# Pairing the first network's up product, and making a third of the later modulations' sums during attention, in a two-layer decoder trunk

## The chip, the cores and the metric

The kernel runs on one core of one Trainium2 chip, as one program and one launch. The metric is device time in microseconds, from the runs of the program on the chip; lower is better. Beside the plain runs there is one profiled execution, from which every row in this document comes. Engine names in the rows are PE (TensorE, matmuls), PEld (TensorE, weight loads), DVE (VectorE), ACT (ScalarE), POOL (GpSimd) and SP (SyncE, which here only issues transfers).

## The reference

One sequence of 256 tokens with 2048 channels goes through two layers. Layer 0 mixes tokens by a causal convolution module, layer 1 by causal stick-breaking attention with 16 heads of 128. Behind each mixer stands a gated network with 5632 inner channels, whose up product is followed by a depthwise causal convolution of width 3. Each of these four sub-layers has its own norm and its own shift, scale and gate, a modulation made from one conditioning vector `c`:

```python
def ada_ln(c, w, b):
    mod = jax.nn.silu(c) @ w + b
    shift, scale, gate = jnp.split(mod, 3, axis=-1)

def conv_ffn(h, up_w, dw_w, dw_b, down_w):
    u = causal_depthwise_conv(h @ up_w, dw_w, dw_b)
    gt, val = jnp.split(u, 2, axis=-1)
    return (jax.nn.silu(gt) * val) @ down_w

for i in range(DEPTH):
    shift, scale, gate = ada_ln(c, mix_mod_w[i], mix_mod_b[i])
    h = rms_norm(x, mix_norm_g[i]) * (1.0 + scale) + shift
    y = conformer_conv_module(...) if i == 0 else stick_breaking_mixer(...)
    x = x + gate * y
    shift, scale, gate = ada_ln(c, ffn_mod_w[i], ffn_mod_b[i])
    h = rms_norm(x, ffn_norm_g[i]) * (1.0 + scale) + shift
    x = x + gate * conv_ffn(h, ffn_up_w[i], ffn_dw_w[i], ffn_dw_b[i], ffn_down_w[i])
return rms_norm(x, final_norm_g)
```

All of it is float32.

## The kernel before, in words

**Tiles.** Activations stand with channels on the 128 partitions and the 256 tokens along the free axis, so `x` is 16 tiles of 128 x 256. A weight matrix is cut into blocks of 128 x 128. Eight blocks make a piece of 512 KB, which SP fetches into a tile `raw`, five pieces ahead of its use. The list `stream` holds the pieces of all products in the order in which they are used.

**Two-part products.** Nearly every product is made with operands split into a high and a low part. ScalarE copies a piece of weights into `wh` (L241), VectorE makes `wl = raw - wh` (L245), three pieces ahead, into a ring of four buffers. The activations have such halves too: `h` for a network's or the attention's input, `g` for the gated inner values, `o` for the heads' outputs. A block then needs weights-high times activation-high, weights-high times activation-low, and weights-low times activation-high. `gemm` has two forms of it:

- three matmuls of 256 columns (L301, L302, L303), all into the same 256 columns of a PSUM bank;
- where `both` is given, two matmuls (L296, L297). The two halves of an activation lie in one tile, and an access pattern reads both as 512 columns, so that one matmul multiplies weights-high by both. The bank then holds the high product in its columns 0 to 255 and the low one in columns 256 to 511, and whoever reads the bank adds them. The weights-low matmul goes into the first 256 columns.

Before the change the first network's up product uses the first form, except that its first four columns of blocks come from another function, `product`, with 258 columns. The first network's down product, attention's products and all of the second network use the second form. The last column of each down product uses the first form in both networks.

**What a network does with its up product.** For a column of 128 channels that is done, `up_done` calls `conv3`: in the second form ScalarE copies the low product out of PSUM (L996) and VectorE adds the high one to it (L997). Then ScalarE applies the first tap (L1000), and VectorE the other two (L1003, twice). When both columns of a pair are there, ScalarE applies SiLU, VectorE multiplies (L1015), ScalarE copies the high half (L1017) and VectorE makes the low half `g` (L1018). Each network runs as up00a, up00b, up01a, down00, up01b, down01 (up10a and so on in the second): 4, 40, 2 and 42 columns of up with 16 blocks each, and two down products of 16 columns with 22 blocks each. In down01 each finished column is added to `x` (L1025 on GpSimd, L1029 on VectorE), squared for the next norm (L401, L405), and scaled and split for the next product (L457, L458).

**Modulations.** The later modulations (network 0's gate, all of the attention's and network 1's) are 1 MB tiles of weights, each 128 outputs x 2048 inputs. GpSimd issues the load into a tile `mraw` (L328), and VectorE multiplies it by the conditioning vector and sums along the row in one instruction (L335). The generator `mods1` takes one step per load, and in a step, once its ring of buffers is full, it also issues the sum of the oldest one. The ring has five buffers in the first network, three elsewhere. Generators like this one stand in the list `fill`; after every piece of a product, `tick` adds the product's rate to a credit, and each whole credit advances `fill` by a step. The table `RATES` gives the rate and the starting credit by the product's name. Before the change one generator with 96 tiles runs in the first network, and one with 16 (network 1's gate) in the second. Attention runs with an empty `fill`.

**Attention.** For each group of four heads come the value product, then the query and key products. Each head's own work is a generator in `side` which advances a step per piece. With `q` and `k` done, PE makes the scores (L1106), ScalarE three functions of them, VectorE `e` and `lg` (L1115, L1116), GpSimd two masks (L1118), ScalarE and VectorE the halves `mh` and `ml` (L1127), PE the cumulative sums (L1131 to L1134), VectorE a subtraction (L1135), ScalarE an exponential, GpSimd two masks (L1139), and PE the product with the values (L1144, L1145). The output product `o` follows; each of its finished columns is added to `x` (L1210, twice) and prepared for network 1 (L401, L457, L458). If the shift of network 1's modulation is there, two columns of it are also split (L468 on ScalarE, L469 on VectorE, 128 x 2); if not, that is made up for in one go as soon as it is.

**Order.** PE, VectorE and ScalarE each run their own instructions in the order in which a scheduler placed them; engines meet at semaphores only. An instruction that waits holds up everything behind it on its engine.

## Time and profile before

| what | value |
| --- | --- |
| median of 3 runs | 2295.64 us (2295.11 to 2296.51) |
| the profiled execution's own time | 2295.03 us |
| its span, first to last instruction | 2293.3 us |
| mean granted TensorE clock over the span | 0.998 |
| bytes moved | 603.16 MB, mean 263 GB/s |
| weights' transfers (SP's queue), share of 16 DMA engines | 57.8% |
| modulations' transfers (GpSimd's queue), share of 16 DMA engines | 16.2% |
| modulation sums (L335) | 152, of which 96 between 431 and 1155 us |

The stages in the span: the convolution module to 407 us, the first network to 1155 us, attention with its output product to 1545 us, the second network to the end.

How to read it: a matmul's duration includes its way through the array, and the next one starts well before it ends. Busy time of PE is therefore no measure of its pace; the time of a stage divided by its number of blocks is. A stage is cut at the first matmul of its product. In the answers by stretch, the number behind an engine's busy time is the count of instructions that touch the stretch.

### The profile page before, as it was taken

Reading aid. Unit: us, or ns where it says so; the run is one execution under the profiler, and the core shown is the slowest. Engines: PE = TensorE matmul, PEld = TensorE weight load, DVE = VectorE, ACT = ScalarE, POOL = GpSimd, SP = SyncE. Lnnn points to the kernel's source line nnn. Section 1 sums busy time; section 2 is a strip of 40 time slices with the busy share of each in tenths; the row PEclk is TensorE's granted clock in tenths of the full one; section 3 lists DMA queues with packets and bytes.
Section 4 is the critical chain, followed back from the end, with each engine's and each line's share of the span. In section 5 each row is a group of like instructions: output and inputs, shape, how many; then the busy total and the mean of one; then the engine's idle time right before and its main releaser. Section 6 shows DMA issues by size and latency. Waiting matters only on the chain.

```text
span 2293.3 us, 37838 instructions
## 1 busy us (share of the span) xinstructions
PE 2259.4 (99%) x14466; PEld 2013.9 (88%) x14466; DVE 1791.2 (78%) x2502; ACT 1218.4 (53%) x1930; POOL 411.6 (18%) x535
## 2 busy tenths in 40 slices
PE   7999999999999999999999999999999999999997
PEld 5888678999998999998898888889888888888887
DVE  7689968989998899999975655778899755777654
ACT  2056655755544455555465555657555544555553
POOL 4058713200002100003421100122000010000031
PEclk9999999999999999999999999999999999999999
DMA  9988798789899989888765555566787665666663
GB/s 396 417 337 305 272 364 348 279 299 336 334 332 347 347 316 331 338 325 306 291 192 161 167 174 174 166 192 232 238 286 283 194 192 185 192 192 185 193 191 111
DMA packets 139144, 603.16 MB, mean 263 GB/s; under 512 B 15441, under 2 KB 15569, under 8 KB 115153
## 3 DMA queue, kind: packets, MB, share of 16 engines
q1 hardware_dynamic: 120242, 464.42, 57.8%
q0 software_dynamic: 18720, 136.32, 16.2%
q8 instruction: 113, 1.85, 0.3%
q14 instruction: 69, 0.57, 0.1%
HBM read 598.58 MB, written 2.10 MB: 262 GB/s over the span
## 4 chain that ended last, share of the span: by engine, by line
PE 87%; DVE 6%; DMA 4%; ACT 1%; issue 1%; POOL 0%; DVEq 0%; SPq 0%; ACTq 0%; POOLq 0%
PE ps L296 33%; PE ps L297 17%; PE ps L302 9%; PE ps L301 9%; PE ps L303 9%; PE ps L694 5%; DMA mraw<-in_mt_mix 3%; DVE mraw L335 3%; DVE wl L245 1%; PE ps L1185 1%; PE ps L1184 1%; PE ps L1186 1%; PE ps L585 1%; DMA mraw<-in_mt_ffn 1%; DMA raw<-in_w_pw 1%
## 5 line engine op out<-in xcount | busy, mean ns | idle before, releaser
L245 DVE TENSOR_TENSOR wl<-raw,wh 128x1024 fp32r<-128x1024 f32 x688 | 848.1, 1239 | 298.7 <-ACT wh L241 294.5
L241 ACT CAST wh<-raw 128x1024 fp32r<-128x1024 f32 x688 | 719.5, 1048 | 663.2 <-PE ps L296 279.6
L296 PE MATMUL ps<-h,wh 128*128 128x512 f32 x1760 | 613.5, 394 | 0.0
L297 PE MATMUL ps<-h,wl 128*128 128x256 f32 x1760 | 488.8, 278 | 0.0
L296 PE MATMUL ps<-g,wh 128*128 128x512 f32 x1320 | 458.1, 392 | 0.0
L303 PE MATMUL ps<-h,wl 128*128 128x256 f32 (+1 forms) x1504 | 423.4, 281 | 0.0
L302 PE MATMUL ps<-h,wh 128*128 128x256 f32 (+1 forms) x1504 | 423.2, 281 | 0.0
L301 PE MATMUL ps<-h,wh 128*128 128x256 f32 (+1 forms) x1504 | 419.8, 279 | 0.0
L296 PEld LDWEIGHTS ps<-h,wh 128*128 128x128 f32 x1760 | 330.4, 188 | 76.3
L335 DVE CUSTOM_DVE_ANT_0 mraw<-mraw,csr 128x2048 f32<-128x2048 f32 x152 | 350.1, 2304 | 32.1 <-DMA mraw<-in_mt_mix 28.6
L297 PE MATMUL ps<-g,wl 128*128 128x256 f32 x1320 | 369.9, 280 | 2.3 <-DVE wl L245 2.2
L297 PEld LDWEIGHTS ps<-h,wl 128*128 128x128 f32 x1760 | 330.5, 188 | 0.2
L296 PEld LDWEIGHTS ps<-g,wh 128*128 128x128 f32 x1320 | 247.8, 188 | 54.7
L301 PEld LDWEIGHTS ps<-h,wh 128*128 128x128 f32 x1504 | 284.2, 189 | 0.1
L303 PEld LDWEIGHTS ps<-h,wl 128*128 128x128 f32 x1504 | 283.0, 188 | 0.4
L302 PEld LDWEIGHTS ps<-h,wh 128*128 128x128 f32 x1504 | 283.1, 188 | 0.1
L297 PEld LDWEIGHTS ps<-g,wl 128*128 128x128 f32 x1320 | 248.6, 188 | 4.2 <-DVE wl L245 4.2
L694 PE MATMUL ps<-h,raw 128*128 128x256 f32 x832 | 188.8, 382 | 0.0
L694 PEld LDWEIGHTS ps<-h,raw 128*128 128x128 f32 x832 | 157.8, 191 | 28.3 <-issue 6.7
L1025 POOL TENSOR_TENSOR x<-x,t 128x256 f32<-128x256 f32 x56 | 70.5, 1260 | 526.8 <-ACT t L1024 526.7
L1003 DVE SCALAR_TENSOR_TENSOR t<-t,par 128x254 f32<-128x254 f32 (+1 forms) x184 | 88.7, 482 | 46.6 <-ACT t L1000 43.7
L734 DVE SCALAR_TENSOR_TENSOR auxb<-u,cpar,auxb 128x256 f32<-128x256 f32 x297 | 121.6, 482 | 4.5 <-ACT auxb L718 3.8
(271 smaller groups left out, 2739.7 us busy)
## 6 DMA issues: line engine op xcount, KB each, us to landing
raw<-in_w_down SPq DMA_DIRECT2D x176, 512.0 KB, 4.2
mraw<-in_mt_ffn POOLq DMA_DIRECT2D x64, 1024.0 KB, 5.8
raw<-in_w_pw SPq DMA_DIRECT2D x96, 512.0 KB, 8.1
mraw<-in_mt_mix POOLq DMA_DIRECT2D x48, 1024.0 KB, 7.7
raw<-in_w_up01b SPq DMA_DIRECT2D x84, 512.0 KB, 6.3
raw<-in_w_up11b SPq DMA_DIRECT2D x84, 512.0 KB, 3.6
raw<-in_w_up00b SPq DMA_DIRECT2D x80, 512.0 KB, 5.7
raw<-in_w_up10b SPq DMA_DIRECT2D x80, 512.0 KB, 4.7
```

What stands on the lines that cost most here:

```text
L241: nc.scalar.copy(wh[:, :n], v[:, :n])
L245: nc.vector.tensor_tensor(wl[:, :n], v[:, :n], wh[:, :n].bitcast(F32), op=ALU.subtract)
L296: nc.tensor.matmul(o, wh[:, c], both[kt], start=first, stop=False, skip_group_check=True)
L297: nc.tensor.matmul(o[:, :T], wl[:, c], xh[kt], start=False, stop=left[nb] == 0, skip_group_check=True)
L301: nc.tensor.matmul(o, wh[:, c], xh[kt], start=first, stop=False, skip_group_check=halves > 0)
L302: nc.tensor.matmul(o, wh[:, c], xl[kt], start=False, stop=False, skip_group_check=halves > 0)
L303: nc.tensor.matmul(o, wl[:, c], xh[kt], start=False, stop=left[nb] == 0, skip_group_check=halves > 0)
L335: nc.vector.tensor_tensor_reduce(out=v, in0=v, in1=csr, scale=1.0, scalar=0.0, op0=ALU.mult, op1=ALU.add, accum_out=macc[:, nb:nb + 1])
L694: nc.tensor.matmul(banks[j][:, nb // KD * T:(nb // KD + 1) * T], w[:, b * P:(b + 1) * P], hf[kt], start=first, stop=left[j] == 0, skip_gro ...
L734: nc.vector.scalar_tensor_tensor(conv_ps[j], us[j % UBUFS][:, k:k + T], tap(j, k), conv_ps[j], op0=ALU.mult, op1=ALU.add)
L1003: nc.vector.scalar_tensor_tensor(y[:, s:], ps[:, :T - s], w(k), y[:, s:], op0=ALU.mult, op1=ALU.add)
L1025: nc.gpsimd.tensor_tensor(xs[nb], xs[nb], t, op=ALU.add)
```

## The change

Three edits:

- In the first network, `both` is now given to up00b, up01a and up01b, and their columns go to `conv3` with `both`. So 84 columns of 16 blocks are made with L296 and L297 instead of L301 to L303, and each column takes the copy L996 and the sum L997 more.
- The generator of 96 modulation tiles ends after 64: network 0's gate and all of the attention's. The other 32, network 1's scale and shift, go to a second generator with a ring of three buffers, which starts when the first network is over and so runs in attention.
- The table of rates: `up` from 0.39 to 0.28, `up00b` from 0.4 to 0.28, `down` from 0.43 to 0.28; `qk` and `v` from 0.3 to 0.42 and `qk0b` from 0.3 to 0.42. With these, 22 steps fall into up00b, 1 into up01a, 12 into down00, 23 into up01b and 10 into down01; of the second generator, 28 steps fall into attention and 7 into the output product, which makes 26 sums there and 6 here.

```diff
-RATES = {"pw2": (1.0, 0.0), "up": (0.39, 0.25), "down": (0.43, 0.0), "qk": (0.3, 0.0), "v": (0.3, 0.0),
+RATES = {"pw2": (1.0, 0.0), "up": (0.28, 0.0), "down": (0.28, 0.0), "qk": (0.42, 0.0), "v": (0.42, 0.0),
...
             hh, hl = entry.product(f"up{i}0a", up_done, "silu_and_others")
-            both = h_pairs() if i else None
-            rest = (lambda nb, ps: up_done(nb, ps, True)) if i else up_done
+            both = h_pairs()
+            rest = lambda nb, ps: up_done(nb, ps, True)
             gemm(f"up{i}0b", hh, hl, rest, banks=[psum_b, psum_a], both=both)
             gemm(f"up{i}1a", hh, hl, rest, both=both)
             need(m, 2)
...
-    fill.append(mods1((("ffn0", 2), ("mix1", 1), ("mix1", 0), ("mix1", 2), ("ffn1", 1), ("ffn1", 0)),
+    fill.append(mods1((("ffn0", 2), ("mix1", 1), ("mix1", 0), ("mix1", 2)),
                       lambda: [mpool] * 3 + [more["pool"]] * MORE_MODS))
     entry1 = Entry("mix1")
     ffn(0, entry, entry1)
+    fill.append(mods1((("ffn1", 1), ("ffn1", 0)), lambda: [mpool] * 3))
```

Lines behind the added one move down by one in the changed kernel (L1115 becomes L1116).

PE at the start of up00b, before the change. A row is the line, the operation, what is written from what, and the size of what is written; `auxb` and `auxa` are PSUM banks, `h_3583` is the tile with both halves of one input tile:

```order
L301 MATMUL auxb<-h_3583,wh 128x256
L302 MATMUL auxb<-h_3583,wh 128x256
L303 MATMUL auxb<-h_3583,wl 128x256
L301 MATMUL auxa<-h_3583,wh 128x256
L302 MATMUL auxa<-h_3583,wh 128x256
L303 MATMUL auxa<-h_3583,wl 128x256
```

The same place after:

```order
L296 MATMUL auxb<-h_3583,wh 128x512
L297 MATMUL auxb<-h_3583,wl 128x256
L296 MATMUL auxa<-h_3583,wh 128x512
L297 MATMUL auxa<-h_3583,wl 128x256
L296 MATMUL auxb<-h_3589,wh 128x512
L297 MATMUL auxb<-h_3589,wl 128x256
```

Two matmuls stand where three stood, with the same 768 columns in all and one weight load less.

VectorE in up00b at the end of a pair of columns, before; `t` are working tiles, `par` the parameters:

```order
L1003 SCALAR_TENSOR_TENSOR t<-ps,par,t 128x254
L1003 SCALAR_TENSOR_TENSOR t<-ps,par,t 128x255
L1015 TENSOR_TENSOR t<-t 128x256
L245 TENSOR_TENSOR wl<-raw,wh 128x1024
L1018 TENSOR_TENSOR g_4875<-t,g_4875 128x256
L335 ISA mraw,macc<-mraw,csr 128x2048
L335 ISA macc 128x1
```

Such a place after:

```order
L997 TENSOR_TENSOR t<-ps,t 128x256
L1003 SCALAR_TENSOR_TENSOR t<-t,par 128x254
L1003 SCALAR_TENSOR_TENSOR t<-t,par 128x255
L1015 TENSOR_TENSOR t<-t 128x256
L245 TENSOR_TENSOR wl<-raw,wh 128x1024
L1018 TENSOR_TENSOR g_4910<-t,g_4910 128x256
L335 ISA mraw,macc<-mraw,csr 128x2048
L335 ISA macc 128x1
```

The sum of the halves comes ahead of the two taps, which now read SBUF and no longer PSUM; the modulation sum stands as before, but there are fewer of them.

VectorE in the last group of heads, around one head's `e`, `lg` and `ml`, before:

```order
L1115 SCALAR_TENSOR_TENSOR e<-auxa,lg 128x384
L1116 SCALAR_TENSOR_TENSOR lg<-auxa,lg 128x384
L245 TENSOR_TENSOR wl<-raw,wh 128x1024
L1161 SCALAR_TENSOR_TENSOR q<-ps,q 128x256
L1127 TENSOR_TENSOR ml<-e,mh 128x384
L1150 TENSOR_TENSOR o_13590<-auxb,o_13590 128x256
L245 TENSOR_TENSOR wl<-raw,wh 128x1024
L1135 TENSOR_TENSOR lg<-lg,auxb 128x384
L1166 TENSOR_TENSOR k<-ps,k 128x256
```

The same head after:

```order
L1116 SCALAR_TENSOR_TENSOR e<-auxa,lg 128x384
L1117 SCALAR_TENSOR_TENSOR lg<-auxa,lg 128x384
L335 ISA mraw,macc<-mraw,csr 128x2048
L335 ISA macc 128x1
L1162 SCALAR_TENSOR_TENSOR q<-ps,q 128x256
L1128 TENSOR_TENSOR ml<-e,mh 128x384
L1151 TENSOR_TENSOR o_13818<-auxb,o_13818 128x256
L245 TENSOR_TENSOR wl<-raw,wh 128x1024 x2
L1136 TENSOR_TENSOR lg<-lg,auxb 128x384
L1167 TENSOR_TENSOR k<-ps,k 128x256
```

A modulation sum now stands between `lg` and `ml`, where one of the weight splits stood, and that split has moved behind `ml`.

More of the change, by code (lines that the diff above doesn't have):

```diff
@@ L38 @@
 ROWS_TAIL = 5
-RATES = {"pw2": (1.0, 0.0), "up": (0.39, 0.25), "down": (0.43, 0.0), "qk": (0.3, 0.0), "v": (0.3, 0.0),
+RATES = {"pw2": (1.0, 0.0), "up": (0.28, 0.0), "down": (0.28, 0.0), "qk": (0.42, 0.0), "v": (0.42, 0.0),
          "o": (0.45, -3.0), "up00a": (0.0, 0.0), "qk0a": (0.0, 0.0),
-         "up00b": (0.4, 0.0), "up10a": (0.0, 0.0), "up10b": (0.25, -2.0), "v0": (0.0, 0.0), "qk0b": (0.3, -1.5)}
+         "up00b": (0.28, 0.0), "up10a": (0.0, 0.0), "up10b": (0.25, -2.0), "v0": (0.0, 0.0), "qk0b": (0.42, -1.5)}
 QUIET = 6
```

## The prediction, made before the changed kernel was run

> **What bounds the kernel now.** The page comes first: the span, the busy shares, and the chain of work that ended last.
>
> ```profile
> span 2293.3 us, 37838 instructions
> PE 2259.4 (99%) x14466; PEld 2013.9 (88%) x14466; DVE 1791.2 (78%) x2502; ACT 1218.4 (53%) x1930; POOL 411.6 (18%) x535
> PE 87%; DVE 6%; DMA 4%; ACT 1%; issue 1%; POOL 0%; DVEq 0%; SPq 0%; ACTq 0%; POOLq 0%
> ```
>
> PE holds 87% of the chain, so the question is its pace, and where something stops it. For that the span is cut by stages; each row gives the stretch, its length, then busy time and instruction count of PE, PEld, DVE, ACT, POOL, then clock and DMA. First the first network (up00b, up01a, down00, up01b, down01), then the second's up10b, up11a, down10, up11b, then attention's last two groups and the output product:
>
> ```profile
> 431.46:658.25 226.79, 226.41 (x1922) 226.20 (x1921) 209.28 (x281) 121.76 (x174) 14.14 (x27) 1.00 0.90 333
> 658.25:669.56 11.31, 11.31 (x98) 11.31 (x97) 10.83 (x13) 5.79 (x8) 1.06 (x2) 1.00 0.80 296
> 669.56:791.67 122.11, 122.11 (x729) 109.12 (x728) 104.61 (x105) 53.53 (x61) 28.71 (x33) 1.00 0.93 350
> 791.67:1029.11 237.44, 237.44 (x2019) 237.44 (x2017) 216.96 (x275) 123.03 (x180) 16.41 (x31) 1.00 0.89 329
> 1029.11:1155.11 126.00, 123.69 (x729) 109.05 (x728) 118.72 (x131) 63.57 (x94) 46.42 (x41) 1.00 0.79 293
> ...
> 1569.36:1792.03 222.67, 222.14 (x1283) 193.76 (x1282) 199.27 (x293) 133.98 (x213) 6.88 (x13) 1.00 0.76 267
> 1792.03:1803.12 11.09, 11.09 (x67) 9.69 (x65) 10.11 (x17) 6.44 (x10) 0.00 (x0) 1.00 0.57 189
> 1803.12:1925.30 122.18, 122.18 (x729) 107.69 (x727) 64.11 (x67) 53.65 (x62) 14.61 (x14) 1.00 0.63 194
> 1925.30:2158.25 232.95, 232.95 (x1346) 203.36 (x1345) 168.82 (x248) 133.55 (x206) 0.00 (x0) 1.00 0.62 190
> ...
> 1304.47:1453.54 149.07, 149.07 (x819) 128.42 (x818) 85.04 (x119) 80.55 (x132) 14.84 (x32) 1.00 0.55 170
> 1453.54:1545.09 91.55, 91.55 (x535) 81.21 (x535) 68.96 (x86) 55.25 (x77) 19.56 (x20) 1.00 0.60 184
> ```
>
> up01b and up11b are the same 672 blocks, once in three matmuls (2019 touching instructions, 3 x 672 and three at the edges), once in two (1346, 2 x 672 and two). A block takes 237.44/672 = 0.3533 us in threes and 232.95/672 = 0.3467 us in twos. The clock is 1.00 in both. The triple stage has PEld busy without a break, the paired one 87% of the time. So the second network is the experiment with the paired form, already in the trace. down01 is the other place: 126.00 us against 122.11 and 122.18 for the same 352 blocks in down00 and down10. In it the waits are:
>
> ```profile
> PE ps L297 <- DVE wl L245: 2.2, 4, 0.7
> PEld ps L297 <- DVE wl L245: 4.2, 6, 1.0
> ```
>
> PE stops there for weights-low halves that VectorE brings too late. VectorE is busy 118.72 of 126.00 us, 94%. In attention it is busy 85.04 of 149.07, 57%.
>
> **The change, part by part.** The sum is made against the profiled execution, 2295.03 us. That is 0.6 under the median of the three runs, which lie 1.4 apart; a measurement of this kernel can tell about 0.2%, 4.6 us, from no change.
>
> *The pairing.* The stages of the second network give the price with everything that comes with the form, copies and sums of halves included: up00b 226.79 to 222.67 (-4.12), up01a 11.31 to 11.09 (-0.22), up01b 237.44 to 232.95 (-4.49). Together -8.8 us. [...] The rows of the two networks show 6.6 ns per block; the measurement decides.
>
> *VectorE in the first network's up stages.* Added are 84 sums of halves, removed from the network 32 modulation sums:
>
> ```profile
> L335 DVE CUSTOM_DVE_ANT_0 mraw<-mraw,csr 128x2048 f32<-128x2048 f32 x152 | 350.1, 2304 | 32.1 <-DMA mraw<-in_mt_mix 28.6 <-DMA mraw<-in_mt_ffn 3.5
> L997 DVE TENSOR_TENSOR t<-ps,t 128x256 f32<-128x256 f32 x82 | 34.2, 417 | 0.0
> L996 ACT COPY t<-ps 128x256 f32<-128x256 f32 x82 | 29.6, 361 | 0.0
> ...
> 1086.15 2.28 DVE L335 CUSTOM_DVE_ANT_0 mraw<-mraw,csr 128x2048 f32<-128x2048 f32 x1
> 1088.36 1.75 DVE L245 TENSOR_TENSOR wl<-raw,wh 128x1024 fp32r<-128x1024 f32 x1
> 1090.03 0.47 DVE L1029 SCALAR_TENSOR_TENSOR x<-ps,v_ffn,x 128x256 f32<-128x256 f32 x1
> 1090.43 1.21 DVE L245 TENSOR_TENSOR wl<-raw,wh 128x1024 fp32r<-128x1024 f32 x1
> 1091.56 0.96 DVE L458 SCALAR_TENSOR_TENSOR h<-x,a_mix,h 128x256 fp32r<-128x256 f32 x1
> ...
> 1086.48 2.55 POOL L1025 TENSOR_TENSOR x<-x,t 128x256 f32<-128x256 f32 x1
> ```
>
> A modulation sum holds VectorE for 2.21 us (1086.15 to the next start at 1088.36). So 32 x 2.21 = 71 us leave, 84 x 0.42 = 35 us come. up01b: 168.82 (up11b has no modulation sums) + 23 x 2.21 = 219.7 of 232.95 us, 94%; up00b: 199.27 with up10b's 15 sums, and 7 more make 214.7 of 222.67, 96%. up01a before stood at 10.83 of 11.31, 96%, and PE never stopped there, so I take 0, with 8 us of cover left in up00b. If that cover were gone, each further us would be PE's; an upper bound is one lost split, 1.1 us. ScalarE adds 84 x 0.36 = 30 us at 53% busy: nothing. Each sum of halves waits for ScalarE's copy, and behind it on VectorE stand the taps and the next split; the second network has the same queue, and in up11b and up11a PE is busy without a break. SP's queue is unchanged, and fewer transfers of GpSimd's pass beside it: nothing, since PE waits for no transfer here.
>
> *down01's relief.* The number of modulation sums there falls from 17 to 10, 15.5 us less on VectorE: 118.72 - 15.5 = 103 of 122 us, 85%, below down00's 104.61 of 122.11, which has 18 sums and no stop. The bounds are 0 (the stops stay: four columns still end together) and 3.9 us (all go). down00 is the nearer row, so I take 3.4.
>
> *Sums in attention.* There are 26 sums, 57 us of VectorE, on stages with 43% idle. Per group of four heads (149.07/2 = 74.5 us) VectorE goes from 42.5 to 42.5 + 10 x 2.21 = 64.6 us, 87%. What counts is the chain of a head, whose margins stand in the timeline; here the head of the quoted order:
>
> ```profile
> 1433.66 0.56 DVE L1116 SCALAR_TENSOR_TENSOR lg<-auxa,lg 128x384 f32<-128x384 f32 x1
> 1434.91 1.23 DVE L245 TENSOR_TENSOR wl<-raw,wh 128x1024 fp32r<-128x1024 f32 x1 [0.69 <-ACT wh L241]
> 1436.06 0.42 DVE L1161 SCALAR_TENSOR_TENSOR q<-ps,q 128x256 f32<-128x256 f32 x1
> 1436.39 0.55 DVE L1127 TENSOR_TENSOR ml<-e,mh 128x384 fp32r<-128x384 f32 x1
> 1441.95 1.43 POOL L1139 TENSOR_SCALAR_AFFINE_SELECT e<-e 128x128 f32<-128x128 f32 x2 [7.66 <-ACT e L1137]
> 1440.17 0.33 PE L1132 MATMUL auxb<-ml,tri_r 128*128 128x384 f32 x1
> 1446.78 0.38 PE L1144 MATMUL auxb<-e,v 128*128 128x128 f32 x2
> L328 POOL DMA_DIRECT2D mraw<-in_mt_ffn x64 | 34.3, 537 | 451.1 <-DVE t L997 192.8 <-DVE t L1003 168.8 <-DVE macc L335 86.6
> ```
>
> `ml` is ready at 1436.94 and PE wants it at 1440.17: 3.2 us. The masks end at 1443.38 and PE wants them at 1446.78: 3.4 us. With one sum (2.21) in place of one split, `ml` starts at about 1434.2 + 2.2 + 0.4 = 1436.8, hardly later than 1436.39. GpSimd's loads of modulations now stand between its masks, and a load that waits holds up the masks behind it and so the head. But each waits for a sum that was issued a step earlier, some 7 us (74.5/10), and costs 0.54 us itself. Nothing is gained in attention, since nothing leaves it; the bounds are 0 and, if each of 16 heads lost 1.4 us (two sums, 4.4 + 0.2, against 3.2), 22 us. The order has one sum there, so I take 0.5.
>
> *Sums in the output product.* Six sums fall into about 13 pieces in its first half.
>
> ```profile
> 1480.94 1.21 DVE L245 TENSOR_TENSOR wl<-raw,wh 128x1024 fp32r<-128x1024 f32 x1
> 1487.07 0.28 PE L297 MATMUL ps<-o,wl 128*128 128x256 f32 x1
> L468 ACT CAST h<-v_ffn x32: 177/188/203, 399.4 to 1454.3; 128x2 fp32r<-128x2 f32 x32
> L469 DVE TENSOR_TENSOR h<-v_ffn,h x32: 144/150/245, 401.5 to 1455.9; 128x2 fp32r<-128x2 f32 x32
> ```
>
> Counted by their order, these two rows are the split and the first use of the same piece, the closest of this product: 4.9 us of margin. VectorE is idle 22.59 of 91.55 us, 0.7 us per piece, 9.1 in 13 pieces; six sums need 13.3. So some 4.2 us of the margin go. Then the shift, ready late, is split for 13 tiles at once: 13 x 0.19 us on ScalarE, on which VectorE waits, some 2 us. 4.9 - 4.2 - 2 is below nothing by 1.3. The bounds are 0 and 3; I take 1.0.
>
> The sum: -8.8 - 3.4 + 0.5 + 1.0 = -10.7, and 2295.03 - 10.7 = **2284.3 us**, 0.5% faster.
>
> **The rivals.**
>
> *The relief does not come.* down01's stops start where four columns end together, and those stay together. With -8.8 + 1.5 the time is 2287.7. Against it speaks down00. Chance 14%.
>
> *Attention pays in small coin.* The POOL row above speaks for it: an add that starts beside a modulation sum takes 2.55 us, until 0.67 us after that sum's end. A mask that meets a sum could be held the same way, and its 3.4 us of margin be eaten together with a late `lg`. Half a us per head is 8 us, so 2291.8: no difference that can be measured. [...] Chance 10%.
>
> *Attention becomes VectorE's.* If heads meet two sums in the stretch to `ml`, each loses 1.4 us, 22 in all: -12.2 + 22 = 2305 us, slower. It decides from a loss of 0.76 us per head on (12.2/16), that is with `ml` 4.0 us later than now. Against it stand the order, with one sum there, and 87% for a group. Chance 4%.
>
> *The short saving.* If the triples' pace is partly the doing of the DMA traffic beside them (a share of 0.89 and 0.90 there, 0.62 and 0.76 in the paired stages), the pairing gives less. At half of 8.8 the time is 2295.03 - 4.4 - 3.4 + 1.5 = 2288.7. Against it speaks that down00 (0.93) and down10 (0.63) differ by 0.07 us. Chance 3%.
>
> **How the numbers follow.** My forecast has 64%, and 5% are left for what I do not see, 3 of them on the faster side. Faster by over 0.2% (under 2291.0) are the forecast, the first rival, the last one, those 3 and a third of the second: 0.87. Within 0.2% is the rest of the second and one more: 0.08. Slower: 0.05. The range starts where all of down01's stops go and the moved sums cost nothing, -12.7, less 0.7 for half the spread of the runs: 2281.6. It ends at 2290.5, which takes in the first rival, the last, and the better half of the second.
>
> **What would show it.** In the profile after: up00b, up01a, up01b at 222.7, 11.1 and 233.0 us with PEld near 87%; down01 near 122.5 with one or two waits of PE for L245; attention's last two groups at 149.1 with VectorE near 85%; the output product near 92.6, with PE waiting for L245 in its second half. It is wrong if up01b stays above 236, if down01 stays near 126, or if PE's rows in attention wait for `ml`, masks or splits for over 4 us together.

## The result, and the profile after

| what | before | after |
| --- | --- | --- |
| median, runs taken beside each other | 2296.07 us (4 runs, 2295.11 to 2301.74) | 2282.66 us (4 runs, 2281.19 to 2285.57) |
| the profiled execution, its span | 2295.03 us, 2293.3 us | 2285.57 us, 2283.9 us |

The ratio of the times is 0.9941, with a 95% interval of 0.9923 to 0.996: faster by 13.4 us where 10.7 were forecast (from 2295.03, not from this batch's 2296.07), and 2282.66 against a forecast of 2284.3. In a later batch the same kernel stood at 2282.66 again (5 runs) beside 2295.06 of the kernel before (17 runs), 12.4 us apart.

The page of the changed kernel: its span, its busy shares and the shares of the chain that ended last.

```profile
span 2283.9 us, 35258 instructions
PE 2251.4 (99%) x13122; PEld 1948.6 (85%) x13122; DVE 1811.8 (79%) x2586; ACT 1245.2 (55%) x2014; POOL 416.8 (18%) x535
PE 89%; DVE 5%; DMA 4%; ACT 1%; issue 1%; POOL 0%; DVEq 0%; SPq 0%; ACTq 0%; POOLq 0%
```

1344 matmuls are gone (14466 to 13122), one for each block of the 84 columns, and PE's share of the chain has risen. Now the stages, in the order up00b, up01a, up01b, down01, attention's last two groups, output product, with the columns as before:

```profile
429.96:656.76 226.80, 226.25 (x1282) 198.12 (x1281) 203.64 (x301) 133.41 (x213) 9.45 (x18) 1.00 0.79 291
656.76:668.07 11.31, 11.31 (x67) 9.91 (x66) 9.56 (x15) 6.47 (x10) 0.53 (x1) 1.00 0.81 302
790.17:1023.15 232.98, 232.98 (x1347) 203.46 (x1346) 210.62 (x296) 135.00 (x221) 11.69 (x22) 1.00 0.81 295
1023.15:1145.26 122.11, 122.11 (x729) 109.11 (x727) 101.22 (x120) 65.97 (x95) 35.01 (x34) 1.00 0.72 241
...
1294.92:1443.99 149.07, 149.07 (x818) 128.43 (x818) 122.70 (x142) 78.63 (x117) 36.61 (x50) 1.00 0.81 296
1443.99:1535.59 91.60, 91.60 (x534) 81.20 (x534) 82.61 (x116) 55.73 (x92) 24.61 (x25) 1.00 0.72 244
```

up01b took 232.98 us, as its twin up11b did (232.95). down01 took 122.11 and has no stop left. Attention and the output product kept their times with VectorE at 82% and 90%. The weight loads are busy 87% of up01b, as expected of the paired form. But up00b took 226.80 us: with 1282 matmuls instead of 1922 it was exactly as long as before. up01a, behind it, stayed at 11.31.

Two numbers outside the change belong to this comparison. The convolution module's second product took 121.25 us here and 122.89 in the profile before, 1.6 us that the last section explains. And the profile's own time, 2285.57, is the highest of its four. So two things are to be tested: whether the steps of the sum hold one by one, and why up00b gained nothing in this execution.

### The profile page after: what moved, and what is told of

The parts are those of the page before. It is cut to its first block, busy times and chain, and to the rows that moved or that the text cites. A ratio compares the mean times of both kernels' runs of the same rounds, so it can differ in the third digit from the quotient of the medians.

```text
span 2283.9 us, 35258 instructions
## 1 busy us (share of the span) xinstructions
PE 2251.4 (99%) x13122; PEld 1948.6 (85%) x13122; DVE 1811.8 (79%) x2586; ACT 1245.2 (55%) x2014; POOL 416.8 (18%) x535
## 4 chain that ended last, share of the span: by engine, by line
PE 89%; DVE 5%; DMA 4%; ACT 1%; issue 1%; POOL 0%; DVEq 0%; SPq 0%; ACTq 0%; POOLq 0%
PE ps L296 47%; PE ps L297 24%; PE ps L694 5%; DMA mraw<-in_mt_mix 3%; PE ps L301 2%; DVE mraw L335 2%; PE ps L302 2%; PE ps L303 2%; PE ps L1186 1%; PE ps L1185 1%; PE ps L1187 1%; DVE wl L245 1%; PE ps L585 1%; DMA raw<-in_w_pw 1%; DMA mraw<-in_mt_ffn 1%
## 5 line engine op out<-in xcount | busy, mean ns | idle before, releaser
L296 PE MATMUL ps<-h,wh 128*128 128x512 f32 x3072 | 1072.9, 394 | 0.0
L297 PE MATMUL ps<-h,wl 128*128 128x256 f32 x3072 | 857.2, 279 | 0.0
L296 PEld LDWEIGHTS ps<-h,wh 128*128 128x128 f32 x3072 | 576.7, 188 | 133.5
L297 PEld LDWEIGHTS ps<-h,wl 128*128 128x128 f32 x3072 | 577.8, 188 | 0.2
L296 PE MATMUL ps<-g,wh 128*128 128x512 f32 x1320 | 457.8, 392 | 0.0
L297 PE MATMUL ps<-g,wl 128*128 128x256 f32 x1320 | 369.3, 280 | 0.0
L296 PEld LDWEIGHTS ps<-g,wh 128*128 128x128 f32 x1320 | 247.7, 188 | 55.0
L297 PEld LDWEIGHTS ps<-g,wl 128*128 128x128 f32 x1320 | 248.7, 188 | 0.0
L1003 DVE SCALAR_TENSOR_TENSOR t<-t,par 128x254 f32<-128x254 f32 x352 | 169.7, 482 | 60.9 <-ACT t L1000 56.1
L1000 ACT ACTIVATE t<-t,par 128x256 f32<-128x256 f32 x176 | 105.9, 602 | 124.2 <-DVE t L997 124.1
L869 POOL TENSOR_TENSOR y<-y,h 128x256 f32<-128x256 f32 x143 | 104.6, 732 | 13.2 <-ACT h L743 3.0
L328 POOL DMA_DIRECT2D mraw<-in_mt_ffn x64 | 34.7, 542 | 371.0 <-DVE t L997 255.0
L405 POOL TENSOR_TENSOR sumsq<-sumsq,t 128x256 f32<-128x256 f32 x56 | 64.0, 1143 | 142.6 <-ACT t L401 142.5
L296 PE MATMUL ps<-o,wh 128*128 128x512 f32 x256 | 89.5, 392 | 0.0
```

The costliest lines, as they stand in the source:

```text
L296: nc.tensor.matmul(o, wh[:, c], both[kt], start=first, stop=False, skip_group_check=True)
L297: nc.tensor.matmul(o[:, :T], wl[:, c], xh[kt], start=False, stop=left[nb] == 0, skip_group_check=True)
L328: nc.gpsimd.dma_start(v, src)
L405: engine.tensor_tensor(self.sum, self.sum, sq, op=ALU.add)
L869: nc.gpsimd.tensor_tensor(ys[c], ys[c], pr, op=ALU.add)
L1000: nc.scalar.activation(y, ps[:, :T], AF.Identity, bias=pc(f"fdb{i}", nb, 1), scale=w(FW - 1))
```

## The experiments

### The same kernel again

No edit. Is up00b always 226.8 us long?

> The changed kernel once more, to see whether up00b keeps the pace that it had in the profiled execution after the change (226.8 us, 0.3533 us per block, although paired), while up01b ran at 0.3467. Theory of the two paces: after PE's stop for VectorE near 439 us the stream of pairs falls into one of two steady rhythms, and which one is chance; then this profile shows up00b at either 222.7 or 226.8 us, nothing between, and the timed runs lie in two heaps some 4 us apart, near 2281 and 2285. Rival, something steady in up00b (its banks, its transfers): 226.8 us again, and all runs in one heap.

2282.66 us (2280.66 to 2284.27, ratio 0.9948, interval 0.9936 to 0.996); the profiled execution took 2282.51. Its up00b, up01a, and attention with the output product:

```profile
431.48:654.17 222.69, 222.15 (x1282) 193.77 (x1281) 202.18 (x300) 132.88 (x213) 9.38 (x18) 1.00 0.81 293
654.17:665.27 11.10, 11.10 (x67) 9.70 (x66) 9.79 (x17) 6.34 (x10) 0.53 (x1) 1.00 0.93 342
...
1142.47:1532.57 390.10, 389.89 (x2214) 340.06 (x2213) 316.48 (x399) 223.22 (x349) 89.70 (x120) 1.00 0.73 259
```

The same program, the same matmuls (1282), the same clock, and up00b is 4.1 us shorter, as forecast. So the paired stage has two paces. The two heaps of times that I expected are not there: the five runs lie at 2280.66, 2282.51, 2282.66, 2283.37 and 2284.27 us. But the two paces show in the starts of matmuls, first in the profiled execution after the change, then in this one; ten blocks lie between the rows of a fence (columns: start, duration, engine, line, operation):

```profile
499.88 0.39 PE L296 MATMUL ps<-h,wh 128*128 128x512 f32 x1
...
503.41 0.39 PE L296 MATMUL ps<-h,wh 128*128 128x512 f32 x1
```

```profile
499.91 0.39 PE L296 MATMUL ps<-h,wh 128*128 128x512 f32 x1
...
503.37 0.39 PE L296 MATMUL ps<-h,wh 128*128 128x512 f32 x1
```

Ten blocks take 3.53 us in the one, 3.46 in the other: 353 and 347 ns for a block, here called the long and the short rhythm. 353 is also the pace of the three-matmul form. No single matmul is longer by its row; the distances are. From 500 to 560 us the 256-column matmul is followed by the next after 121 ns on average in the first execution and 116 in the second, the 512-column one after 232.5 and 231.

### The pairing alone

```diff
-RATES = {"pw2": (1.0, 0.0), "up": (0.28, 0.0), "down": (0.28, 0.0), "qk": (0.42, 0.0), "v": (0.42, 0.0),
+RATES = {"pw2": (1.0, 0.0), "up": (0.39, 0.25), "down": (0.43, 0.0), "qk": (0.3, 0.0), "v": (0.3, 0.0),
...
-    fill.append(mods1((("ffn0", 2), ("mix1", 1), ("mix1", 0), ("mix1", 2)),
+    fill.append(mods1((("ffn0", 2), ("mix1", 1), ("mix1", 0), ("mix1", 2), ("ffn1", 1), ("ffn1", 0)),
...
-    fill.append(mods1((("ffn1", 1), ("ffn1", 0)), lambda: [mpool] * 3))
```

All 96 sums stay in the first network (the other two rates of the table also go back).

> The pairing alone: all 96 sums stay in the first network at the old rates. VectorE would then need in up00b 199.3 + 12 x 2.21 = 225.8 us of 222.7, in up01b 168.8 + 32 x 2.21 = 239.5 of 233.0. Theory that VectorE is the next bound there: the two stages take about 226 and 239.5 us with PE waiting for L245, down01 stays at 126 or above, and the kernel lies within 3 us of the kernel before (2293 to 2298). Rival, that VectorE's work overlaps better than its busy time says: up01b at 233, down01 at 126, in all 4 to 9 us faster than before (2287 to 2292).

2286.85 us (ratio 0.9966, interval 0.9954 to 0.9978), 8.2 less than before. up00b, up01a, up01b and down01, and what PE waits for in down01:

```profile
432.03:654.71 222.68, 222.14 (x1282) 193.75 (x1281) 217.19 (x318) 133.37 (x213) 14.15 (x27) 1.00 0.90 334
654.71:665.80 11.09, 11.09 (x66) 9.68 (x65) 11.09 (x15) 6.49 (x10) 0.54 (x1) 1.00 0.93 345
787.92:1020.90 232.98, 232.98 (x1347) 203.46 (x1345) 225.84 (x312) 134.53 (x221) 16.41 (x31) 1.00 0.90 331
1020.90:1147.53 126.63, 123.93 (x728) 108.99 (x727) 121.12 (x137) 64.12 (x95) 47.40 (x41) 1.00 0.82 300
```

```profile
PE ps L297 <- DVE wl L245: 2.5, 4, 0.7
```

My theory, that VectorE would bind the paired up stages with all sums left there, fell. VectorE is busy 97% of up00b and up01b and all of up01a, and PE stops in them only once, for 0.5 us early in up00b, as it does in every profile. Only down01 keeps its stops, 126.63 us. The pairing is worth its whole price without the move; the move is worth what down01 loses.

### The move alone

```diff
-            both = h_pairs()
-            rest = lambda nb, ps: up_done(nb, ps, True)
+            both = h_pairs() if i else None
+            rest = (lambda nb, ps: up_done(nb, ps, True)) if i else up_done
```

> The moved sums and the new rates alone, the first network's up product in three matmuls as before. Theory: down01 falls from 126.0 to 122.1 us by the relief of VectorE alone, up00b and up01b stay at 226.8 and 237.4, attention and the output product cost 0.4 us; 3.5 us faster than before (2292.5). Rival, that the relief in down01 comes with the pairing: down01 stays near 126 and the kernel is as before or 0.4 slower.

2291.25 us (11 runs; ratio 0.9986, interval 0.9977 to 0.9995), 3.8 less than before. down01, and attention with the output product:

```profile
1027.56:1149.67 122.11, 122.11 (x729) 109.12 (x727) 100.16 (x117) 65.61 (x94) 35.58 (x34) 1.00 0.71 242
1149.67:1539.79 390.12, 389.91 (x2215) 340.07 (x2213) 316.48 (x399) 223.20 (x349) 89.73 (x120) 1.00 0.73 259
```

up00b and up01b stand at 226.80 and 237.44 as before, all of the gain is down01's 126.00 to 122.11, and attention gives nothing back. The two halves of the change add up: 8.2 + 3.8 = 12.0 of 12.4.

### Without the moved sums

```diff
-    fill.append(mods1((("ffn1", 1), ("ffn1", 0)), lambda: [mpool] * 3))
+    for part in (1, 0):
+        mod_sum("ffn1", part * KD, KD)
+        if part == 1:
+            mod_scale("ffn1", 0, KD)
+        have.add(("ffn1", part))
```

The loads and sums of 32 tiles are left out, so network 1's shift and scale hold other values.

> The changed kernel without the 32 modulation tiles of attention: neither their loads nor their sums are made, so network 1's shift and scale hold other values. It gives the price of the moved work. By the two profiles attention with its output product went from 389.98 to 390.33 us, so the theory expects 0.3 us less than the changed kernel, with up00b in either of its two paces. Rival, that the moved work costs time that those two stretches do not show (transfers beside the second network's start, later stages): more than 2 us less than the changed kernel at the same pace of up00b.

2283.97 us (2281.01 to 2290.97, ratio 0.996, interval 0.9946 to 0.9973): no less than with them. Attention with the output product, then up10b, up11a and down10 of the profiled execution, which took 2290.97:

```profile
1144.20:1534.19 389.99, 389.78 (x2215) 340.00 (x2213) 250.06 (x332) 224.84 (x349) 55.28 (x88) 1.00 0.53 173
1558.44:1785.24 226.80, 226.25 (x1282) 198.12 (x1281) 199.56 (x294) 134.22 (x213) 6.88 (x13) 1.00 0.74 262
1785.24:1796.55 11.31, 11.31 (x67) 9.91 (x65) 10.12 (x16) 6.45 (x10) 0.00 (x0) 1.00 0.60 185
1796.55:1920.92 124.37, 124.37 (x728) 110.06 (x727) 63.91 (x67) 53.83 (x62) 14.36 (x14) 1.00 0.60 190
```

389.99 against 390.10 with the sums in the repetition and 390.33 in the first profile: 66 us of VectorE's work and 32 MB of traffic cost 0.1 to 0.3 us there. And the long rhythm came back in a place that the change does not touch. Here the second network's up10b had it, in an execution whose up00b took 222.69 us, and handed it on through up11a and down10: 4.1 + 0.2 + 2.2 = 6.5 us. The traffic was 262 GB/s against 267 in the profile before, where the same stage kept the short rhythm.

### The moved sums twice

```diff
             mod_reduce(m, nb, v)
             behind(on)
+            if m == "ffn1" and part < 2:
+                on = last_of(nc.vector.engine)
+                mod_reduce(m, nb, v)
+                behind(on)
```

Each of the 32 sums is made twice, so that those modulation values differ.

> The changed kernel with every moved modulation sum made twice, so network 1's shift and scale hold other values. It tests how much room VectorE has in attention. By the prediction's budget a group of four heads needs 42.5 + 20 x 2.21 = 86.7 us of VectorE in 74.5 us of PE's time, so the last two groups take 12 us more each and the output product 10 more; some 35 to 40 us slower than the changed kernel in all. Rival, that attention hides VectorE's work in time that the budget counts twice, as up01b did with the pairing alone: under 10 us slower.

2331.96 us (ratio 1.0164, interval 1.0145 to 1.0183), 49.3 more than the changed kernel. Attention and the output product, and PE's largest waits in them:

```profile
1144.10:1468.91 324.81, 305.57 (x1677) 257.96 (x1675) 278.16 (x326) 167.76 (x257) 67.49 (x95) 1.00 0.68 238
1468.91:1582.42 113.51, 99.63 (x540) 84.34 (x539) 103.79 (x137) 57.11 (x93) 25.36 (x26) 0.97 0.61 209
```

```profile
PE ps L297 <- DVE wl L245: 9.5, 7, 1.7
PE auxb L1149 <- POOL e L1144: 7.1, 7, 1.4
PE auxb L1151 <- POOL e L1144: 6.2, 9, 1.6
```

Against the repetition these are 26.3 us more in attention and 21.9 in the output product, and in all more than the 35 to 40 expected. The first sum of a step is nearly free (0.1 to 0.3 us for all of them) and a second one is paid for. PE waits for splits, and for GpSimd's masks (L1144 in this kernel's numbering). In the last twelve heads these masks take 1.5 to 2.9 us, no longer than in the changed kernel; what is late is their start. In the head whose masks begin at 1444.64 us, VectorE comes to the subtraction ahead of them (L1140) only at 1443.46, 4.7 us after the end of the cumulative sums, behind a modulation sum and two splits; in the profile after it starts the subtraction 0.03 to 0.04 us behind them in each of the 16 heads.

### What sets the rhythm

In the profile after, the long rhythm begins right behind a stop of PE early in up00b:

```profile
438.29 0.40 PE L296 MATMUL auxb<-h,wh 128*128 128x512 f32 x1
439.24 0.39 PE L297 MATMUL auxb<-h,wl 128*128 128x256 f32 x1 [0.55 <-DVE wl L245]
```

Before it, a block takes 347 ns; behind it, 353 ns through up00b and up01a, until down00 begins. A stop of PE for a split stands early in up00b in every profile of the paired form (0.54 us in the repetition), mostly with the short rhythm behind it. Three kernels put more matmuls into the stream to see what such a stop does. In the first, every eighth piece of the four long up stages holds one more matmul of 128 columns, into a bank that nobody reads, which needs the newest `wl`; these are 42, not the 40 that I had counted:

```diff
         for blocks, wh, wl in pieces(name):
+            stop_at = name in ("up00b", "up01b", "up10b", "up11b") and todo % 8 == 1
             for b, (nb, kt) in enumerate(blocks):
+                if stop_at and b == 5:
+                    late = psum_a()
+                    nc.tensor.matmul(late[:, :P], parts[-1][2][:, :P], xh[0][:, :P], start=True, stop=True)
```

> The changed kernel with 40 short stops of PE: in up00b, up01b, up10b and up11b, every eighth piece, one more matmul of 128 columns reads the newest weights-low half, which VectorE is just making, and writes a bank that nobody reads. Theory of the two paces (a stop's end decides the rhythm): the 40 stretches behind the stops run at 0.3467 or 0.3533 us per block, nothing between, a few of them (some 3 to 15 of 40) at 0.3533, in the second halves of the networks too, and a stretch keeps its pace until the next stop. Rival, that the slow pace belongs to the start of a network (its banks, its clock): all 40 stretches behind the stops at 0.3467.

2301.08 us in one run; its time is that of the stops and says nothing else. Of the 42 stretches behind them, 40 have 347 ns for a block and 2 have 353. One of the two starts at the matmul at 570.43 us (L284); ten blocks again lie between the first two rows, the next two, and the last two, which stand behind the next stop:

```profile
565.66 0.39 PE L300 MATMUL ps<-h,wh 128*128 128x512 f32 x1
...
569.13 0.39 PE L300 MATMUL ps<-h,wh 128*128 128x512 f32 x1
...
570.43 0.33 PE L284 MATMUL auxa<-h,wl 128*128 128x128 f32 x1
...
573.95 0.39 PE L300 MATMUL ps<-h,wh 128*128 128x512 f32 x1
...
577.48 0.39 PE L300 MATMUL ps<-h,wh 128*128 128x512 f32 x1
...
593.70 0.39 PE L300 MATMUL ps<-h,wh 128*128 128x512 f32 x1
...
597.16 0.39 PE L300 MATMUL ps<-h,wh 128*128 128x512 f32 x1
```

3.47, 3.53, 3.46 us for ten blocks: a stop begins the long rhythm, the next one ends it, and nothing between does. I had thought of 3 to 15 such stretches. The length of a stop does not tell the first one apart: a distance of 262 ns behind a 512-column matmul had the long rhythm behind it, 261 and 267 the short one. For the other, at 871.90 us, that is open: its 151 ns are the shortest of the distances behind a 256-column matmul, the next being 183.

That other long stretch ended at an added matmul that did not stop PE:

```profile
894.38 0.40 PE L300 MATMUL ps<-h,wh 128*128 128x512 f32 x1
894.61 0.23 PE L284 MATMUL auxa<-h,wl 128*128 128x128 f32 x1
894.68 0.33 PE L301 MATMUL ps<-h,wl 128*128 128x256 f32 x1
```

It starts 0.23 us behind the 512-column matmul, as any undisturbed one does, and ten blocks take 3.47 us from there on. So the long rhythm can end without a stop.

In the second kernel the extra matmul reads the piece's own `wl`, and so does not wait:

```diff
-                    nc.tensor.matmul(late[:, :P], parts[-1][2][:, :P], xh[0][:, :P], start=True, stop=True)
+                    nc.tensor.matmul(late[:, :P], wl[:, :P], xh[0][:, :P], start=True, stop=True)
```

> The same 40 extra matmuls, but each reads a weights-low half that is long there, so PE does not stop. Theory that only a stop draws the rhythm: each stage keeps the pace that it had ahead of the extra matmuls, and 40 x 0.12 = 5 us at most are added. Rival, that any irregularity draws it: paces change behind some of them without a stop.

2289.13 us, one run. All 42 stretches have 347 ns: no added matmul without a wait began the long rhythm. But at the first kernel's rate of 2 in 42, none in 42 would come by chance in 13 of 100 such runs (an estimate). That the wait begins the long rhythm, and not the added matmul, is likely by this and is not shown. As no long stretch came up here, the run says nothing of what ends one.

In the third, two blocks behind each stop (b = 5 and 6) are made in three matmuls, in the hope that this always brings the short rhythm:

```diff
-                    nc.tensor.matmul(o, wh[:, c], both[kt], start=first, stop=False, skip_group_check=True)
+                    if stop_at and b in (5, 6):
+                        nc.tensor.matmul(o[:, :T], wh[:, c], xh[kt], start=first, stop=False, skip_group_check=True)
+                        nc.tensor.matmul(o[:, T:], wh[:, c], xl[kt], start=False, stop=False, skip_group_check=True)
+                    else:
+                        nc.tensor.matmul(o, wh[:, c], both[kt], start=first, stop=False, skip_group_check=True)
```

> The same 40 stops, but the two blocks that follow each stop take three matmuls of 256 columns, into the same columns of the bank. If the rhythm is set by how the first pairs meet the weight loads after a stop, three-matmul blocks in between let it start anew without a stop: all 40 stretches at one pace, 0.3467 by hope, for 2 x 6.6 ns each. Rival, that any irregularity draws the rhythm anew: a mixture as in the run with plain stops.

2301.70 us, one run. The hope fell: 9 of 42 stretches have 353 ns. With the change of form behind the stop the long rhythm was more frequent, 9 against 2 in one execution each.

### Three tries to keep the short rhythm

If the early stop of up00b is the danger, either the stop must go or it must fall elsewhere. Two kernels give GpSimd 6 or 7 of 8 of the entry's tiles instead of 5, to have VectorE's splits earlier:

```diff
-                            self.h[kt] = modulate_tile(self.m, kt, self.rs, pool=kt % 8 < 5)
+                            self.h[kt] = modulate_tile(self.m, kt, self.rs, pool=kt % 8 < 6)
```

> The changed kernel with 12 of 16 input tiles of each later stage scaled on GpSimd in place of 10, which takes some 2 x 0.9 us of work off VectorE just ahead of PE's stop near 439 us (and its twin in the second network). Theory: the stop of 0.55 us shrinks or goes in both networks, about 1 us less at the same rhythms (2281.5 median), and with no stop there is no draw, so up00b and up10b stand at 222 us and no run lies near 2285 or above. Rival, that GpSimd becomes the late one there (its tiles take about 1 us each): the stop moves or grows, same time or up to 3 us slower.

2283.36 us (5 runs, ratio 0.9939, interval 0.9924 to 0.9953): the stop stayed (0.49 us), and v0 behind the attention's entry grew from 22.40 to 23.24 us.

> The same with 14 of 16 tiles on GpSimd. Theory: no stop of PE for L245 in the first 12 us of up00b and up10b, at the price of GpSimd's longer row of tiles ahead of up00b's start: 0 to 1.5 us less than the changed kernel. Rival, GpSimd late: PE waits for the last input tiles at the start of up00b, 1 to 4 us slower in each of three places.

With 7 of 8, 2289.77 us (8 runs, ratio 0.9967, interval 0.9954 to 0.998): up00b 225.04, up10b 225.05 and v0 23.76 us. These are 2.3, 2.3 and 1.4 us more than in the repetition, the price that the rival named for a late GpSimd. But PE does not wait for input tiles, as the rival had it: early in up00b it waits 1.0 us for ScalarE's copy of weights and 1.3 us for two splits, and what makes these late is open. The third kernel makes the first two columns of up00b and up10b in three matmuls, so that the stop falls into those:

```diff
+                    self.head = up[FIRST:FIRST + 2]
...
-            gemm(f"up{i}0b", hh, hl, rest, banks=[psum_b, psum_a], both=both)
+            gemm(f"up{i}0b", hh, hl, lambda nb, ps: up_done(nb, ps, nb not in cfg.head), banks=[psum_b, psum_a], both=both,
+                 apart=cfg.head)
```

> The changed kernel with the first two columns of up00b and up10b (32 blocks each, in which PE's stop falls) in three matmuls and only then pairs. By the stops with three-matmul blocks behind them, of which at least 9 of 42 went to the slow rhythm against 2 of 42 for plain stops, I expect no safe start from this: the pairs behind start with the rhythm drawn at the change of form, up00b at 222.9 or 227.0 us. Rival, that without a stop among pairs the rhythm is always the fast one: 222.9 us in both networks and all timed runs below 2284.

2282.71 us (5 runs, ratio 0.9937, interval 0.9922 to 0.9951). up00b took 222.72 and up10b 222.74 in its profile. One profile cannot say whether that is always so, and the time is the changed kernel's. None of the three beats it.

## Why the prediction was right, and where it was not

| step | forecast | profile after | the same kernel again |
| --- | --- | --- | --- |
| up00b paired | -4.12 | 0.0 | -4.09 |
| up01a paired | -0.22 | 0.0 | -0.22 |
| up01b paired | -4.49 | -4.46 | -4.46 |
| down01's relief | -3.4 | -3.89 | -3.89 |
| sums in attention | +0.5 | +0.3 | +0.1 |
| sums in the output product | +1.0 | +0.05 | +0.03 |
| sum | -10.7 | -8.0 | -12.5 |

The first profiled execution was 9.5 us faster than the one before, of which 1.6 are the convolution module's. That this lies so near the forecast is luck: a saving of 4.3 us did not come, and the last three steps came out 1.6 us better. In the repetition only these last three differ from the forecast, by 1.9 us.

**The pairing.** The second network's rows gave the price to 0.03 us, whenever the short rhythm ran; the pairing alone measures -8.2 by medians, where -8.8 was forecast. What failed is that up00b's price was taken as sure. It was read from one execution of up10b, and a paired stage can also run at 353 ns, which no row of the profile before shows. Over the eight profiles of a paired up00b without the added matmuls it did so once, and up10b once in ten. The price was 4.3 us in the first network and 6.5 in the second.

**VectorE in the up stages.** Nothing, as taken. The load was put too high: for up00b the sum took all 22 steps for sums, but the first steps of a ring only load, and the trace has 18 sums there. In the repetition VectorE was busy 202.18 us in up00b and 210.60 in up01b, not 214.7 and 219.7, so that 20 us were free in up00b and not 8; the last section has the other reason. The pairing alone shows how far this holds: with 27 and 32 sums VectorE is still idle for 5.5 us of up00b and 7.1 of up01b, and beyond the early stop PE loses nothing. What happens when that cover is gone was not tried.

**down01's relief.** All 3.89 us came, the bound and not the 3.4. The rival that the relief does not come is out by the move alone, which gains just this.

**The sums in attention.** The forecast looked at the chain of a head, and the margins that it named are what changed; the price was 0.1 to 0.3 us, under its 0.5. In the head of the quoted order, VectorE's rows and PE's use of `ml`:

```profile
1437.63 2.30 DVE L335 CUSTOM_DVE_ANT_0 mraw<-mraw,csr 128x2048 f32<-128x2048 f32 x1
...
1440.20 0.54 DVE L1128 TENSOR_TENSOR ml<-e,mh 128x384 fp32r<-128x384 f32 x1
```

```profile
1443.65 0.33 PE L1133 MATMUL auxb<-ml,tri_r 128*128 128x384 f32 x1
```

`ml` ends at 1440.74, 2.9 us before its use, where it was 3.2: one sum takes the place of one split, as the order said. The masks are what pays. Two rows of another head, VectorE's sum and GpSimd's two masks, then that head's masks before the change:

```profile
1419.20 2.28 DVE L335 CUSTOM_DVE_ANT_0 mraw<-mraw,csr 128x2048 f32<-128x2048 f32 x1
```

```profile
1419.33 3.53 POOL L1140 TENSOR_SCALAR_AFFINE_SELECT e<-e 128x128 f32<-128x128 f32 x2 [6.40 <-ACT e L1138]
```

```profile
1428.87 1.49 POOL L1139 TENSOR_SCALAR_AFFINE_SELECT e<-e 128x128 f32<-128x128 f32 x2 [6.99 <-ACT e L1137]
```

3.53 us, where the same head had 1.49: the masks lose 2.0 us, nearly the sum's 2.28. So what the second rival thought possible is there: a sum meets the masks in nine of the 16 heads, and those of the other seven took 0.54 to 1.42 us. In eight of the nine it takes 2 us of a margin of 3.4, and 1.2 to 1.4 are left, so that PE does not wait for a mask. With doubled sums the masks are among PE's waits, though they take no longer there: they start late, as said above. The "point from which it decides" was the right question, and the answer lies between one sum per step and two.

**The sums in the output product.** The term of 1.0 was too large. The expected loss of margin is there, at another piece. Counted by their order, these are the split and the first use of the product's 25th piece, VectorE's row and PE's, before the change:

```profile
1515.79 1.23 DVE L245 TENSOR_TENSOR wl<-raw,wh 128x1024 fp32r<-128x1024 f32 x1 [0.67 <-ACT wh L241]
1523.13 0.28 PE L297 MATMUL ps<-o,wl 128*128 128x256 f32 x1
```

The same piece after, the closest of the product now, with what follows its split on VectorE:

```profile
1512.24 1.21 DVE L245 TENSOR_TENSOR wl<-raw,wh 128x1024 fp32r<-128x1024 f32 x1
1513.38 0.47 DVE L1211 SCALAR_TENSOR_TENSOR x<-ps,v_mix,x 128x256 f32<-128x256 f32 x1
1513.78 1.00 DVE L469 TENSOR_TENSOR h<-v_ffn,h 128x2 fp32r<-128x2 f32 x13
```

```profile
1513.58 0.33 PE L297 MATMUL ps<-o,wl 128*128 128x256 f32 x1
```

1513.45 to 1513.58 leaves 0.1 us, where this piece had 6.1. The sum took its 4.2 and 2 us from the 4.9 of the piece that was closest before, the 12th, and that one keeps its 4.9, since all but one of the modulation sums come after its split. The step that failed is the choice of the piece: 6.2 us were charged, 6.0 were lost, but where 6.1 were at hand. The split of the shift for 13 tiles, charged with 2 us, takes 1.00 and stands behind this split; the next piece keeps 0.5 us. That 0.1 us was left, and PE did not wait, is luck as far as the sum goes. Seven sums begin in this stretch and 25 in attention, not 6 and 26.

**The rest.** The fourth rival priced a saving that is half eaten, by traffic. A saving was eaten in up00b, but traffic is not the cause: the stage moved 291 GB/s with the long rhythm and 293 with the short one, and 334 with the short one in the pairing alone.

## What to carry to other kernels

A twin stage in the same trace priced this change of form to 0.03 us per stage, but one execution shows one draw: look at a stage's pace per block in several profiles before calling its price sure. For work moved under a stage, ask not how busy the engine becomes but how much margin each user keeps, and find with a doubled dose where the margin ends. When an interleaving costs 0.1 to 0.3 us at one sum per step and 49 us more at two, it should be noted beside the rate that sets it.

## What the runs showed of the hardware

**Two rhythms of one stream.** A stream of paired matmuls (512 and 256 columns, each with its own weight load) runs at 347 or 353 ns for a block. Where the long rhythm was seen to begin in an undisturbed product, it was at a stop of PE (0.55 us in both cases), and it lasted until the stream was broken, by an added matmul or by another product (down00 in one profile, up11b in another). 2 of 42 added matmuls that mostly stopped PE gave 353, and none of 42 without a wait. The clock (1.00) and the weight loads' share are the same in both (198.12 of 226.80 and 193.77 of 222.69 us, 87%), the traffic nearly so (291 and 293 GB/s). Why the stream has two is open, and so is what decides between them.

**Stretches at half clock.** The profiles differ in one more place, which the change does not touch. At the end of the convolution module's second product, PE waits 1.7 to 1.8 us for `rows` (L601), and the clock granted behind this wait differs. The row of the profile before, then after, then two successive rows of the kernel without the moved sums:

```profile
398.19:402.19 4.00, 4.00 (x24) 4.00 (x23) 4.00 (x13) 2.10 (x9) 0.80 (x1) 0.59 1.03 410
```

```profile
396.71:400.71 4.00, 4.00 (x36) 4.00 (x37) 4.00 (x6) 2.54 (x11) 1.07 (x1) 1.00 1.02 410
```

```profile
395.94:399.94 4.00, 3.56 (x17) 3.56 (x18) 3.92 (x6) 2.57 (x9) 1.25 (x1) 0.57 1.02 411
399.94:403.94 4.00, 4.00 (x23) 4.00 (x23) 3.38 (x10) 1.71 (x6) 0.00 (x0) 0.57 0.92 367
```

The product took 122.89, 121.25 and 124.44 us. In pieces of 1 us the clock is 0.50 within such a stretch and 1.00 around it. So the first row, 4.0 x (1 - 0.59) = 1.64 us lost, holds 3.3 us at half clock; the two rows of the kernel without the moved sums, 8.0 x (1 - 0.57) = 3.44 us lost, hold 6.9 us of it without a break. Each such stretch is a step of 1.6 us in the three times. Of the ten profiles without added matmuls three have none, five have one (1.68 to 1.72 us lost by the row and the one ahead of it) and two have two (3.44 us). What decides between none, one and two was not shown. With these steps and the two rhythms, the two profiles of the changed kernel can be told: 2285.57 has the long rhythm (+4.3) and no such stretch, 2282.51 the short one and one stretch (+1.6); of the 3.1 us between them that is 2.7. What the timed runs had is not known, since they have no profile. Some runs of the kernel before at 2299.9 to 2303.4 us have no explanation here.

**Busy time of a stage with gaps.** A row's end overlaps the next row's start: the split of 1.21 us above starts at 1512.24 and the next instruction at 1513.38, 1.14 us on. A stretch's busy time counts such an overlap once. In up00b of the pairing alone the 318 rows of VectorE last 240.6 us together, the busy time is 217.19, and VectorE is idle for the other 5.5 us; 97% busy is 97% taken. A row with idle time behind it counts in full, however, and added work fills such gaps. That is one reason why 168.82 us of up11b and 32 sums of 2.21 us did not make the 239.5 us that the pairing alone was expected to need in up01b, but 225.84: 102 of up11b's 248 rows overlap the next one and 278 of up01b's 312. Without the 64 rows of the sums these are 112 overlaps more, at some 0.08 us each 9 us of the 13.7, an estimate from these two traces. The prediction took 2.21 for 2.28 us for the modulation sum, but added it to the busy time of stages with gaps.
